# Shift and scale of the first norm in four tiles of 512 columns, each followed by its early projection units

## The chip, the cores and the metric

The kernel runs on one core of a Trainium2 chip. The core has TensorE (PE: matmuls; its weight loads are listed as PEld), VectorE (DVE), ScalarE (ACT), GpSimd (POOL) and SyncE (SP, which here only issues DMAs), and 16 DMA engines that move data between HBM and the on-chip memory. Each engine works through its own queue in order and waits at an instruction until the semaphores of that instruction are met. The metric is the device time of one execution in microseconds.

## The reference

One layer of a decoder trunk on 256 tokens of width 2048, in float32: a mixer with four groups of attention heads, and a mixture of 16 experts. Only the beginning matters here:

```python
c_act = silu(c)                                   # (1, 2048)
mod = c_act @ ada_w + ada_b                       # (1, 12288)
sh1, sc1, g1, sh2, sc2, g2 = split(mod, 6)
h = rmsnorm(x, norm1_g) * (1 + sc1) + sh1         # (256, 2048)
x = x + g1 * token_mixer(h, w_in, ...) 
h = rmsnorm(x, norm2_g) * (1 + sc2) + sh2
x = x + g2 * moe_ffn(h, ...)
return rmsnorm(x, final_g)
```

`token_mixer` multiplies h with w_in (2048 rows) and `moe_ffn` runs every token through two of 16 experts; all experts' weights are read, 201 MB of the 368 MB that come from HBM. The shift sh1 and the scale sc1 are each a product of one row with a 2048 x 2048 matrix (16.8 MB each).

## The kernel before

**Order of the work.** Weights come through one stream of units of 512 KB (class `Stream`): a list `units`, in which each entry has a key and a DMA that SyncE issues. They go through a ring of 11 slots (RING). `stream.get` hands out a unit, `stream.done` gives its slot back, and the next unit of the list is then issued into that slot; later more buffers join the free list. The instructions of the program are then put in order for each engine by a scheduler that works with an estimate of its own, so the rows of an engine's queue don't stand in the order of the source.

**The first stage** computes the hidden activations h, transposed, in 16 tiles k of 128 rows by 256 tokens, and starts the projection with w_in as soon as tiles of h exist.

- `ada_acc` (lines 457 to 475) computes a tile of shift or scale: for each unit it multiplies the row silu(c) (spread over 32 columns, `cB`) with 128 rows of ada_w. Four matmuls for four k go to four column groups of TensorE at a time (`tile_position`), and ScalarE copies the sums out into `ada_ev`. In the trace a float32 matmul has two records, so that four matmuls make two packs of four.
- `ada_cols` (lines 488 to 504) adds the four groups and turns the row into columns: the column matmuls (tile `ada_c`, L498), a transpose on VectorE (L500), and the bias (L501).
- `hidden` (lines 599 to 604): hs = xT * A1 + B1 on VectorE, the high half Hh on ScalarE, the low half Hl on VectorE.
- `halves` (lines 555 to 566) splits a unit of w_in into high and low parts, whi on ScalarE (L560, 1048 ns) and wlo on VectorE (L562, 1225 ns). There are two buffers of each (SPLITS).
- `early_mms` and `early_mms5` multiply such a unit with the tiles of h: three matmuls of 256 columns for each product (lines 537 to 539), 24 for a unit, into accumulators that stay in PSUM. 16 units of the first kind (`uwe`, one k each, 1024 columns of w_in) and 7 of the second (`uw`, four k each, 256 columns) are done in this stage: 552 matmuls.
- `x_transposes` (lines 592 to 597) makes xT, and `bias_tiles` (lines 525 to 532) makes the tables of the relative-position bias, 16 small matmuls a time, and needs nothing else.

Shift and scale come in eight tiles of 256 columns, that is two k each. A unit of such a tile holds 512 rows of 256 columns, in pieces of 1 KB. The loop over j (lines 606 to 637) does a scale tile, then a shift tile, then `hidden(j)`, and sets the early units of the tiles before in between. Behind the stage come the gates of the fourth head group (`gacc`, L680), the rest of the projection, attention, the output projection, the router, and from about 563 us on the experts in pairs.

Of the kernel before, what the change touches and what calls it, by code (L numbers as in the profile page):

```python
# [36 lines left out]
SIXTH = 6  # L37
ATAG = "ada"
# [111 lines left out]
def hybrid_trunk_kernel(  # L150
# [34 lines left out]
    def ada_units(col, key, n, kn):  # L185

        def mk(u):
            return lambda t: nc.sync.dma_start(
                t.rearrange("p (k n) -> p k n", k=kn), adaT[:, kn * u:kn * u + kn, col:col + n])
        return [((key, u), mk(u)) for u in range(KC // kn)]  # L190
# [8 lines left out]
    def win_units(i):  # L199
        m, kind, j, col = wtiles[i]  # L200
        if kind == "g":
            return [((("w", i), 0), lambda t: nc.sync.dma_start(
                t[:, 0:384].rearrange("p (k n) -> p k n", k=KC), winT[:, :, col:col + 24]))]

        def mk(u):
            return lambda t: nc.sync.dma_start(
                t.rearrange("p (k n) -> p k n", k=4), winT[:, 4 * u:4 * u + 4, col:col + 256])
        return [((("w", i), u), mk(u)) for u in range(4)]
# [43 lines left out]
    def early_unit(k):  # L252
        return (("we", k), lambda t: nc.sync.dma_start(t, winT[:, k, 3840:4864]))
# [1 line left out]
    acol = {"sh1": 0, "sc1": 2048, "g1": 4096, "sh2": 6144, "sc2": 8192, "g2": 10240}  # L255

    def ada_tile(key):
        return ada_units(acol[key[0]] + 256 * key[1], key, 256, 4)

    def ada_block(key):  # L260
        nm, b, width = key
# [4 lines left out]
                                              [(nm, 2 * h, 512), (nm, 2 * h + 1, 512)])]  # L266

    units = []
    for j in range(8):
        units += ada_tile(("sc1", j))  # L270
        if j == 0:
            units += [(None, lambda t=t: nc.sync.dma_start(x0[t], x[0, 128 * t:128 * t + 128, :])) for t in range(2)]
        units += [early_unit(2 * j)] + ada_tile(("sh1", j)) + [early_unit(2 * j + 1)]
        if j % 2:
            units.append(win_units(4)[j // 2])
        elif j:
            units.append(win_units(SIXTH)[j // 2 - 1])

    nw = len(wtiles)
    wkeys = [u[0] for i in range(NEARLY, nw) for u in win_units(i)[3 * (i == SIXTH):]]  # L280
# [287 lines left out]
    def early_split(k):  # L568
        esp[k] = halves(stream.get(("we", k)))
        stream.done(("we", k))  # L570

    def early_mms(k):
        hi, lo = esp.pop(k)
        for i in range(4):
            for cc in range(2):
                c0 = 256 * i + 128 * cc
                three(early[i][:, cc, :], hi[:, c0:c0 + 128], lo[:, c0:c0 + 128], Hh[:, k, :], Hl[:, k, :],
                      False, k == KC - 1 and cc == 1, True)
# [24 lines left out]
            A.copy(Hh[:, k, :], hs[:])  # L603
            V.tensor_tensor(Hl[:, k, :], hs[:], Hh[:, k, :].bitcast(F32), OP.subtract)

    for j in range(8):
        ev = None
        for u in range(4):
            ev = ada_acc(("sc1", j), [u], ev, 4, 256)
        if j == 0:  # L610
            norm1()
        else:
            early_mms(2 * j - 2)
        x_transposes(2 * j)
        bias_tiles(2 * j)
        ada_cols(ev, 2, A1[:, 2 * j:2 * j + 2], 16 + 2 * j, g1n[:, 2 * j:2 * j + 2], tag=ATAG)
        early_split(2 * j)
        ev = None
        for u in range(4):
            ev = ada_acc(("sh1", j), [u], ev, 4, 256)  # L620
        bias_tiles(2 * j + 1)
        ada_cols(ev, 2, B1[:, 2 * j:2 * j + 2], 2 * j, tag=ATAG)
        hidden(j)
        if j:
            early_mms(2 * j - 1)
        if j and j % 2 == 0:
            early_mms5(4, j // 2 - 1)
        early_split(2 * j + 1)
        if j % 2:
            if j > 1:  # L630
                early_mms5(SIXTH, j // 2 - 1)
            early_split5(4, j // 2)
        elif j:
            early_split5(SIXTH, j // 2 - 1)
    for k in (14, 15):
        early_mms(k)
    early_mms5(4, 3)


    qkv = {}  # L640
# [567 lines left out]
    i = -1  # L1208
# [434 lines left out]
```

## Time and profile before

| | us |
|---|---|
| median of 3 runs (lowest, highest) | 1061.38 (1059.71, 1063.89) |
| the profiled execution | 1063.05 |
| its span, first to last instruction | 1061.3 |
| busy in the span: TensorE | 965.6 (91%) |
| VectorE | 516.6 (49%) |
| ScalarE | 330.6 (31%) |
| data moved | 371.18 MB, mean 350 GB/s |

The profile gives for each engine the time in which it executes something; waiting is idle time. Matmuls overlap, and their ends are modelled, so that the distance between starts tells more than the duration of one. The granted clock (PEclk) is the share of TensorE's 2.4 GHz that it was allowed; 0.50 is 1.2 GHz. The DMA share is the sum of the packets' times over the 16 engines and can come out a little over 1. Tiles are named with the stream's names: `usc` and `ush` are units of the scale and the shift, `uwe` and `uw` units of w_in.

### The profile page before, as it was taken

The numbers are of one execution on the slowest core, as the hardware profiler recorded it, in microseconds if no ns is written. First come the engines' busy times: TensorE is split into PE (matmuls) and PEld (weight loads), VectorE is DVE, ScalarE is ACT, GpSimd is POOL, SyncE is SP. The second block draws the span as 40 slices with busy tenths as digits, with TensorE's granted clock in tenths as the row PEclk, the third lists the DMA queues.
The fourth block names the chain that finished last, engine by engine and source line by source line (L and its number), as shares of the span: only waits on it lengthen the run. The fifth ranks groups of instructions, "written<-read, shape, count | busy, mean of one in ns | idle before, by whom it ended". The sixth has DMA issues, their size and how long they took to land.

```text
span 1061.3 us, 16623 instructions
## 1 busy us (share of the span) xinstructions
PE 965.6 (91%) x6433; PEld 587.5 (55%) x6433; DVE 516.6 (49%) x1093; ACT 330.6 (31%) x710; POOL 4.8 (0%) x14
## 2 busy tenths in 40 slices
PE   5999989899889999979998999999989896998884
PEld 1677778898778986646794434433343332432222
DVE  2444557996899999544345232414133130413115
ACT  3333334455565757634334100100020000200013
POOL 0000000000000000000000000000000000000000
PEclk9999999899989999989998999999999999999997
DMA  9999999996999999999743999999999999999994
GB/s 330 356 358 358 353 318 304 332 360 217 318 352 327 334 348 385 349 304 382 274 150 114 410 408 409 409 409 409 409 409 409 409 408 409 409 410 409 409 387 135
DMA packets 172031, 371.18 MB, mean 350 GB/s; under 512 B 13561, under 2 KB 92322, under 8 KB 171690
## 3 DMA queue, kind: packets, MB, share of 16 engines
q1 hardware_dynamic: 170944, 368.42, 94.6%
q10 hardware_dynamic: 938, 1.61, 0.4%
q8 instruction: 53, 0.87, 0.3%
q14 instruction: 32, 0.26, 0.1%
q0 software_dynamic: 64, 0.02, 0.0%
HBM read 367.91 MB, written 2.10 MB: 349 GB/s over the span
## 4 chain that ended last, share of the span: by engine, by line
PE 57%; DMA 28%; DVE 8%; ACT 3%; issue 3%; SPq 0%; DVEq 0%; ACTq 0%
DMA ugu<-in_exp_w_up_dram 10%; DMA ugu<-in_exp_w_gate_dram 7%; PE dn L170 7%; PE acc L537 5%; PE acc L538 4%; PE acc L539 4%; DMA udh<-in_exp_w_down_dram 4%; PE ada L170 3%; PE gatep L170 3%; PE upp L170 3%; PE oacc L541 3%; PE oacc L542 3%; PE oacc L543 3%; DMA uw<-in_w_in_dram 2%; PE pg L1381 2%
## 5 line engine op out<-in xcount | busy, mean ns | idle before, releaser
L537 PE MATMUL acc<-Hh,wlo 128*128 128x256 f32 x512 | 148.2, 300 | 6.6 <-DVE wlo L562 4.2
L538 PE MATMUL acc<-Hl,whi 128*128 128x256 f32 x512 | 147.4, 290 | 0.0
L539 PE MATMUL acc<-Hh,whi 128*128 128x256 f32 x512 | 146.6, 289 | 0.0
L173 PE MATMUL gatep<-ugu,xg 128*64 128x512 f32 x364 | 122.6, 600 | 0.0
L173 PE MATMUL upp<-ugu,xg 128*64 128x512 f32 x368 | 121.2, 595 | 0.0
L170 PE MATMUL dn<-udh,heT 128*64 128x512 f32 x242 | 112.1, 600 | 2.9 <-DVE heT L1451 2.6
L537 PEld LDWEIGHTS acc<-Hh,wlo 128*128 128x128 f32 x512 | 98.7, 198 | 18.9 <-DVE wlo L562 6.7
L173 PE MATMUL dn<-udh,heT 128*64 128x512 f32 x234 | 108.3, 600 | 0.0
L538 PEld LDWEIGHTS acc<-Hl,whi 128*128 128x128 f32 x512 | 100.2, 196 | 3.4 <-issue 2.9
L539 PEld LDWEIGHTS acc<-Hh,whi 128*128 128x128 f32 x512 | 99.7, 195 | 2.5 <-issue 2.2
L1434 DVE TENSOR_TENSOR he<-upp,sg 128x128 f32<-128x128 f32 x32 | 7.1, 284 | 170.6 <-PE upp L173 167.9
L562 DVE TENSOR_TENSOR wlo<-uw,whi 128x1024 fp32r<-128x1024 f32 x62 | 75.7, 1221 | 15.8 <-ACT whi L560 15.6
L170 PE MATMUL gatep<-ugu,xg 128*64 128x512 f32 x144 | 75.2, 611 | 7.6 <-DMA ugu<-in_exp_w_gate_dram 7.6
L170 PE MATMUL upp<-ugu,xg 128*64 128x512 f32 x144 | 73.6, 600 | 7.8 <-DMA ugu<-in_exp_w_up_dram 7.8
L560 ACT CAST whi<-uw 128x1024 fp32r<-128x1024 f32 x62 | 64.8, 1047 | 48.7 <-PE acc L539 21.4
L1464 DVE TENSOR_TENSOR xt<-xt,sco 128x512 f32<-128x512 f32 (+1 forms) x70 | 42.3, 639 | 54.7 <-PE sco L1463 54.2
L1513 ACT CAST yhl<-yo 128x512 fp32r<-128x512 f32 x31 | 19.2, 618 | 159.7 <-DVE yo L1507 153.3
L170 PEld LDWEIGHTS dn<-udh,heT 128*64 128x64 f32 x242 | 30.0, 136 | 62.1 <-issue 49.1
L562 DVE TENSOR_TENSOR wlo<-uo,whi 128x1024 fp32r<-128x1024 f32 x31 | 37.8, 1223 | 51.2 <-ACT whi L560 49.4
L541 PE MATMUL oacc<-wlo,Oh 128*128 128x512 f32 (+1 forms) x160 | 57.8, 362 | 0.0
L542 PE MATMUL oacc<-whi,Ol 128*128 128x512 f32 (+1 forms) x160 | 56.0, 350 | 0.0
L543 PE MATMUL oacc<-whi,Oh 128*128 128x512 f32 (+1 forms) x160 | 55.9, 350 | 0.0
(397 smaller groups left out, 1730.0 us busy)
## 6 DMA issues: line engine op xcount, KB each, us to landing
ugu<-in_exp_w_up_dram SPq DMA_DIRECT2D x128, 512.0 KB, 10.2
ugu<-in_exp_w_gate_dram SPq DMA_DIRECT2D x127, 512.0 KB, 10.2
udh<-in_exp_w_down_dram SPq DMA_DIRECT2D x119, 512.0 KB, 10.2
usc<-in_ada_w_dram SPq DMA_DIRECT2D x64, 512.0 KB, 7.8
ush<-in_ada_w_dram SPq DMA_DIRECT2D x62, 512.0 KB, 7.1
uw<-in_w_in_dram SPq DMA_DIRECT2D x62, 512.0 KB, 6.0
ug<-in_ada_w_dram SPq DMA_DIRECT2D x56, 512.0 KB, 7.2
uo<-in_w_out_dram SPq DMA_DIRECT2D x31, 512.0 KB, 9.6
```

Of the source, the lines that this page charges most:

```text
L170: ins = op(*args, **kw).ins
L173: ins = op(*args, **kw).ins
L537: ins = mm(o, wl, hh, start=first, stop=False)
L538: mm(o, wh, hl, start=False, stop=False)
L539: mm(o, wh, hh, start=False, stop=last)
L541: ins = mm(o, hh, wl, start=first, stop=False)
L542: mm(o, hl, wh, start=False, stop=False)
L543: mm(o, hh, wh, start=False, stop=last)
L560: A.copy(hi, w)
L562: V.tensor_tensor(lo, w, hi[:].bitcast(F32), OP.subtract)
L1381: mm(pg[:, i, :], x_[:, t, i, 128 * c:128 * c + 128], oh4[q][:, t].rearrange("p e s -> p (e s)"), start=n == 0, stop=n == 3)
L1464: V.tensor_tensor(y(t, cs), y(t, cs), o, OP.add)
```

## The change

The tiles of shift and scale become 512 columns wide, four of each. A unit of 512 KB then holds 256 rows of 512 columns, in pieces of 2 KB, and `ada_acc` takes two units at a time, since four k are needed for the four column groups. In the stream, all 16 units of a tile's scale and shift now come first, and its four units `uwe` and one or two units `uw` follow. The early work becomes a generator, `early_work(j)`, of which the loop takes one piece after each two units of shift or scale of the next tile; what is left is taken before `hidden`. The numbers of matmuls in the early work, of transposes, of bias tiles and of bytes stay as they are.

```diff
     def ada_tile(key):
-        return ada_units(acol[key[0]] + 256 * key[1], key, 256, 4)
+        return ada_units(acol[key[0]] + 512 * key[1], key, 512, 2)
...
-    for j in range(8):
+    for j in range(4):
         units += ada_tile(("sc1", j))
...
-        units += [early_unit(2 * j)] + ada_tile(("sh1", j)) + [early_unit(2 * j + 1)]
-        if j % 2:
-            units.append(win_units(4)[j // 2])
-        elif j:
-            units.append(win_units(SIXTH)[j // 2 - 1])
+        units += ada_tile(("sh1", j)) + [early_unit(k) for k in range(4 * j, 4 * j + 4)]
+        units += [win_units(i)[j] for i in (4, SIXTH)[:2 - (j == 3)]]
...
-    for j in range(8):
+    def early_work(j):
+
+        for k in range(4 * j, 4 * j + 4):
+            early_split(k)
+            yield
+            early_mms(k)
+        for i in (4, SIXTH)[:2 - (j == 3)]:
+            early_split5(i, j)
+            yield
+            early_mms5(i, j)
+        yield
+
+    work = iter(())
+    for j in range(4):
         ev = None
-        for u in range(4):
-            ev = ada_acc(("sc1", j), [u], ev, 4, 256)
+        for u in range(0, 8, 2):
+            ev = ada_acc(("sc1", j), [u, u + 1], ev, 2, 512)
+            next(work, None)
...
+        for _ in work:
+            pass
+        hidden(2 * j)
+        hidden(2 * j + 1)
+        work = early_work(j)
```

How the queues move, at three places. First SyncE at the start of the program: before, four units of the scale, x, one unit of w_in and four units of the shift.

```order
L188 DMA usc_94<-in_ada_w_dram 128x4x256
L188 DMA usc_96<-in_ada_w_dram 128x4x256
L188 DMA usc_98<-in_ada_w_dram 128x4x256
L188 DMA usc_100<-in_ada_w_dram 128x4x256
L272 DMA x_76<-in_x_dram 128x2048
L272 DMA x_77<-in_x_dram 128x2048
L253 DMA uwe_104<-in_w_in_dram 128x1024
L188 DMA ush_106<-in_ada_w_dram 128x4x256
L188 DMA ush_108<-in_ada_w_dram 128x4x256
L188 DMA ush_110<-in_ada_w_dram 128x4x256
L188 DMA ush_112<-in_ada_w_dram 128x4x256
L253 DMA uwe_114<-in_w_in_dram 128x1024
```

Now eight units of the scale stand ahead of x, and the shift's units follow; these are its rows from x on.

```order
L272 DMA x_76<-in_x_dram 128x2048
L272 DMA x_77<-in_x_dram 128x2048
L188 DMA ush_112<-in_ada_w_dram 128x2x512
L188 DMA ush_114<-in_ada_w_dram 128x2x512
L188 DMA ush_116<-in_ada_w_dram 128x2x512
L188 DMA ush_202<-in_ada_w_dram 128x2x512
L188 DMA ush_204<-in_ada_w_dram 128x2x512
L188 DMA ush_212<-in_ada_w_dram 128x2x512
L188 DMA ush_210<-in_ada_w_dram 128x2x512
L253 DMA uwe_220<-in_w_in_dram 128x1024
L188 DMA ush_218<-in_ada_w_dram 128x2x512
L253 DMA uwe_228<-in_w_in_dram 128x1024
```

The first unit of w_in has moved from behind x to behind the seventh unit of the shift, and the first four shift units from place 10 to 13 to places among 13 to 21.

Second, TensorE at the end of a shift tile. Before, behind the column matmuls (`ada_c`) of the fifth shift tile:

```order
L498 MATMUL ada_c<-ada_ev,kc 32x64 x4
L170 MATMUL ada<-usc_779,cB 32x256
L173 MATMUL ada<-usc_779,cB 32x256 x3
L596 MATMUL xtr<-ident,x_76 128x128
L596 MATMUL xtr<-ident,x_77 128x128
L596 MATMUL xtr<-ident,x_76 128x128
L596 MATMUL xtr<-ident,x_77 128x128
L537 MATMUL acc<-Hh,wlo 128x256 x4
L170 MATMUL ada<-usc_785,cB 32x256
L173 MATMUL ada<-usc_785,cB 32x256 x3
```

Now, behind those of the second shift tile; the bias matmuls (`S<-tabs,line`) go on like this to 16 of them:

```order
L173 MATMUL ada<-ush_523,cB 32x512 x2
L495 MATMUL ada_c<-ada_ev,kc 32x128 x4
L526 LDWEIGHTS line
L526 MATMUL S<-tabs,line 128x32
L526 LDWEIGHTS line
L526 MATMUL S<-tabs,line 128x32
```

and these rows follow the sixteenth:

```order
L526 LDWEIGHTS line
L526 MATMUL S<-tabs,line 128x32
L534 MATMUL acc<-Hh,wlo 128x256 x4
L535 MATMUL acc<-Hl,whi 128x256
L536 MATMUL acc<-Hh,whi 128x256
L534 MATMUL acc<-Hh,wlo 128x256
L535 MATMUL acc<-Hl,whi 128x256
L536 MATMUL acc<-Hh,whi 128x256
```

Before, units of the next scale tile and transposes of x stood between the column matmuls and the next split matmuls; now 16 bias matmuls stand there, and the next scale units come 60 split matmuls later or more.

Third, VectorE behind the third shift tile, from the transpose of the columns on (`hs` is the hidden tile before it is split, `Hl` its low half):

```order
L497 STREAM_TRANSPOSE ada_ev<-ada_c 128x128
L498 TENSOR_TENSOR B_173<-ada_ev,rT 128x4
L599 TENSOR_SCALAR hs<-xT,A_172,B_173 128x256 x2
L529 COPY TA<-S 128x16x8
L559 TENSOR_TENSOR wlo<-uwe_1003,whi 128x1024
L601 TENSOR_TENSOR Hl<-hs,Hh 128x256 x2
L529 COPY TC<-S 128x16x8
L599 TENSOR_SCALAR hs<-xT,A_172,B_173 128x256 x2
L559 TENSOR_TENSOR wlo<-uw_1041,whi 128x1024
L601 TENSOR_TENSOR Hl<-hs,Hh 128x256 x2
```

Four tiles of `hs` are now made one after another where there were two, and a bias copy (TA) and a split (wlo) stand between the first two and their low halves.

## Rows read from the trace of the kernel before

**Rows 1.** Busy time of each engine in stretches of the span, with the number of instructions; then granted clock, DMA share and GB/s.

```profile
63.00:147.00 84.00, 78.90 (x943) 60.31 (x940) 38.60 (x87) 29.58 (x57) 0.31 (x1) 1.00 1.05 343
160.00:200.00 40.00, 36.54 (x375) 32.42 (x364) 33.69 (x71) 17.04 (x32) 1.05 (x2) 0.91 0.96 320
200.00:240.00 40.00, 40.00 (x335) 36.26 (x336) 38.41 (x72) 21.83 (x52) 0.00 (x0) 1.00 0.99 345
520.00:580.00 60.00, 55.86 (x367) 45.18 (x367) 32.79 (x77) 27.06 (x53) 0.00 (x0) 0.91 0.42 141
600.00:1000.00 400.00, 369.99 (x1690) 141.99 (x1684) 105.54 (x205) 36.58 (x61) 0.00 (x0) 0.99 1.03 409
```

In each row: the stretch, its length, and the busy times of PE, PEld, DVE, ACT and POOL in that order.

**Rows 2.** Groups of TensorE's matmuls from 63 to 147 us: count, busy time, mean ns of one, idle time before them and what ended most of it.

```profile
L538 PE MATMUL acc<-Hl,whi 128*128 128x256 f32 x120 | 34.0, 290 | 0.0
L539 PE MATMUL acc<-Hh,whi 128*128 128x256 f32 x120 | 33.4, 286 | 0.0
L537 PE MATMUL acc<-Hh,wlo 128*128 128x256 f32 x120 | 32.5, 293 | 0.1
L170 PE MATMUL ada<-usc,cB 128*32 128x256 f32 x40 | 12.0, 390 | 2.5 <-DVE ada_ev L500 2.5
L498 PE MATMUL ada_c<-ada_ev,kc 128*32 128x64 f32 x83 | 3.4, 231 | 1.1 <-ACT ada_ev L474 1.1
```

**Rows 3.** Timeline of TensorE in the same stretch: start, duration.

```profile
86.52 0.28 PE L538 MATMUL acc<-Hl,whi 128*128 128x256 f32 x1
86.64 0.28 PE L539 MATMUL acc<-Hh,whi 128*128 128x256 f32 x1
86.85 0.40 PE L170 MATMUL ada<-usc,cB 128*32 128x256 f32 x1
...
87.09 0.38 PE L170 MATMUL ada<-usc,cB 128*32 128x256 f32 x1
...
87.42 0.39 PE L538 MATMUL acc<-Hl,whi 128*128 128x256 f32 x1
87.64 0.28 PE L539 MATMUL acc<-Hh,whi 128*128 128x256 f32 x1
...
94.01 0.38 PE L170 MATMUL ada<-ush,cB 128*32 128x256 f32 x1
...
94.22 0.38 PE L170 MATMUL ada<-ush,cB 128*32 128x256 f32 x1
```

**Rows 4.** Waits of SyncE's queue from 25 to 147 us: who was waited for, us in total, times, longest.

```profile
SPq L188 <- PE ada L173: 30.6, 26, 6.2
```

**Rows 5.** Timeline of TensorE: the gate matmuls behind the early work.

```profile
159.39 1.93 PE L680 MATMUL gacc<-Hh,uw 128*24 128x256 f32 x32
```

**Rows 6.** DMA from 63 to 130 us, in all and by issues (count, size, median us from issue to landing), and the stretch 400 to 420 us as in rows 1.

```profile
DMA packets 20618, 23.87 MB, mean 356 GB/s; under 512 B 722, under 2 KB 19512, under 8 KB 20609
ush<-in_ada_w_dram SPq DMA_DIRECT2D x17, 512.0 KB, 8.3
usc<-in_ada_w_dram SPq DMA_DIRECT2D x16, 512.0 KB, 9.5
uwe<-in_w_in_dram SPq DMA_DIRECT2D x8, 512.0 KB, 8.6
uw<-in_w_in_dram SPq DMA_DIRECT2D x4, 512.0 KB, 9.6
400.00:420.00 20.00, 19.07 (x134) 13.07 (x132) 19.80 (x49) 14.76 (x35) 0.00 (x0) 1.00 1.05 387
```

**Rows 7.** The start: a shift transfer in the chain of waits (start, duration), the first steady split matmul in the timeline, and a group of split matmuls from 31 to 42.6 us, the first of the three lines.

```profile
11.61 11.92 DMA ush<-in_ada_w_dram
...
33.53 0.39 PE L538 MATMUL acc<-Hl,whi 128*128 128x256 f32 x1
...
L537 PE MATMUL acc<-Hh,wlo 128*128 128x256 f32 x16 | 4.7, 331 | 0.0
```

**Rows 8.** Timeline of TensorE at the gate g1 of the mixer, whose tiles have 512 columns already: start, duration.

```profile
440.56 0.59 PE L170 MATMUL ada<-ug,cB 128*32 128x512 f32 x1
...
440.98 0.59 PE L170 MATMUL ada<-ug,cB 128*32 128x512 f32 x1
```

**Rows 9.** Timeline of all engines behind the last shift tile; in brackets the idle time before and what ended it.

```profile
146.65 0.32 PE L498 MATMUL ada_c<-ada_ev,kc 128*32 128x64 f32 x8 [0.54 <-ACT ada_ev L474]
...
149.13 1.17 PE L537 MATMUL acc<-Hh,wlo 128*128 128x256 f32 x4 [2.17 <-ACT Hh L603]
...
150.06 1.23 DVE L562 TENSOR_TENSOR wlo<-uw,whi 128x1024 fp32r<-128x1024 f32 x1 [0.53 <-ACT whi L560]
150.10 0.41 PE L538 MATMUL acc<-Hl,whi 128*128 128x256 f32 x1
...
150.31 0.42 PE L539 MATMUL acc<-Hh,whi 128*128 128x256 f32 x1
```

**Rows 10.** Four short stretches, columns as in rows 1: the two with idle time, and the two behind them.

```profile
146.20:149.10 2.90, 0.32 (x8) 0.16 (x8) 1.72 (x5) 0.80 (x3) 0.00 (x0) 1.00 1.19 308
149.50:152.50 3.00, 3.00 (x16) 3.00 (x16) 2.48 (x4) 0.83 (x2) 0.00 (x0) 0.50 1.05 379
43.80:46.00 2.20, 0.77 (x9) 0.31 (x10) 2.17 (x7) 0.93 (x2) 0.00 (x0) 1.00 1.09 348
46.90:50.00 3.10, 3.10 (x32) 2.29 (x32) 1.37 (x4) 0.97 (x3) 0.00 (x0) 0.50 1.06 362
```

More of the change, by code (lines that the diff above doesn't have):

```diff
@@ L604, in hidden @@
             V.tensor_tensor(Hl[:, k, :], hs[:], Hh[:, k, :].bitcast(F32), OP.subtract)
-    for j in range(8):
+    def early_work(j):
[10 more added lines that the diff above has]
+    for j in range(4):
         ev = None
-        for u in range(4):
-            ev = ada_acc(("sc1", j), [u], ev, 4, 256)
+        for u in range(0, 8, 2):
+            ev = ada_acc(("sc1", j), [u, u + 1], ev, 2, 512)
+            next(work, None)
         if j == 0:
             norm1()
[L612 to L617, printed above, removed]
-        ev = None
[L619 to L637, printed above, removed]
+        x_transposes(4 * j)
+        x_transposes(4 * j + 2)
+        bias_tiles(4 * j)
+        bias_tiles(4 * j + 1)
+        ada_cols(ev, 4, A1[:, 4 * j:4 * j + 4], 16 + 4 * j, g1n[:, 4 * j:4 * j + 4], tag=ATAG)
+        ev = None
+        for u in range(0, 8, 2):
+            ev = ada_acc(("sh1", j), [u, u + 1], ev, 2, 512)
+            next(work, None)
+        bias_tiles(4 * j + 2)
+        bias_tiles(4 * j + 3)
+        ada_cols(ev, 4, B1[:, 4 * j:4 * j + 4], 4 * j, tag=ATAG)
+        for _ in work:
[3 more added lines that the diff above has]
+        work = early_work(j)
+    for _ in work:
+        pass
     qkv = {}
```

## The prediction

> **What bounds the kernel now.** I read the views in this order: the busy time by stretches, the groups of TensorE in one stretch, the timeline of TensorE instruction by instruction, and SyncE's waits. The change touches the first 160 of 1061.3 us only, so the question is what paces that stage and whether a shift of its end reaches the end of the program.
>
> The stretches [rows 1] show two engines at their limit at once. From 63 to 147 us TensorE is busy 78.90 of 84 us and the DMA engines have a share of 1.05. The groups [rows 2] say what fills TensorE: 360 split matmuls (three lines of 120), the matmuls of shift and scale, the bias tiles. The idle time ahead of them is small: 2.5 us before the first matmul of a scale tile, 1.1 us before the column matmuls, 5.1 us in all (84 less 78.90). The timeline [rows 3] confirms that this is no artefact of long modelled ends: split matmuls start every 0.12 us, and the shift and scale matmuls every 0.24 or 0.22 us in packs of four, without a hole. So TensorE has next to no slack, and SyncE agrees: its longest wait in this stage is for TensorE to release a shift or scale buffer, 30.6 us in 26 waits [rows 4]. DMA is full as well, but any gain in its rate makes it the one that waits.
>
> Behind it, a shift of this stage is kept: 160 to 200 us has TensorE at 36.54 and VectorE at 33.69 of 40, 200 to 240 us has 40.00 and 38.41 [rows 1]. From 520 to 580 us DMA mostly idles (share 0.42), as the expert pass has not begun, and from 600 to 1000 us it streams expert weights at 409 GB/s with a share of 1.03 [rows 1]. That block of fixed length starts when the early and middle stages are done. A microsecond won or lost at 160 us therefore moves the end by about one.
>
> **The change part by part.** The marker for the sum is the gate matmul at 159.39 us [rows 5], which in both orders stands right behind the early projection work.
>
> *Transfers.* The 64 units of shift and scale go from rows of 1 KB to rows of 2 KB. From 63 to 130 us 45 units (23.87 MB) moved [rows 6]; 8 of them have rows of 4 KB, as the expert weights have, and at 409 GB/s take 1.28 us each; the other 37 are left 56.7 us, 1.5 us each. From 400 to 420 us, where all units have rows of 2 KB, 387 GB/s [rows 6] makes 1.35 us. So 64 x 0.15 = 9.9 us of DMA time go away. I count none of it: TensorE has only the 5.1 us of idle time to give, and those are counted below.
> The Trainium skill, "DMA: Bandwidth & Descriptors" (Specifications), puts the least transfer for line rate at 512 B; by it 1 KB and 2 KB rows are equally fast and this term would be 0 in place of 9.9. The trace disagrees, 356 against 387 GB/s; with the rule, the faster rival below would lose half its chance.
>
> *Start.* The first shift tile is complete only after 16 units, not 8. Before, its third unit lands at 23.53 [rows 7], the fourth 1.5 us later at 25.0, and the split matmuls run steadily from 33.53, 8.5 us behind. Now 8 more units precede (8 x 1.35 = 10.8) and the old 8 are cheaper (8 x 0.16 = 1.3): 34.5, and steady from 43.0. By then the kernel before has done 48 split matmuls [rows 7], 16 on each of the three lines up to 42.6 us, the changed one 5; both have done 16 units of shift and scale. 43 x 0.118 = 5.1 us behind, less one group of bias matmuls that the new order has already done (0.5): **+4.6 us**.
>
> *Matmuls of shift and scale.* Half as many, twice as wide. At 512 columns packs start 0.42 us apart [rows 8], twice the 0.22 of 256 columns, so the columns cost the same: 0. What is saved is changing over between kinds of work. In [rows 3] the step from a split matmul to a scale one is 0.21 in place of 0.12, the step back 0.33 in place of 0.22 to 0.24, and the next split matmul follows after 0.22 in place of 0.12: 0.3 us for two changes. In the order of the two programs I count 107 changes between 42.6 us and the last early matmul before, 67 after: 40 x 0.15 = **-6.0 us** (half to one and a half times that are my bounds).
>
> *Tile boundaries.* Before, the first matmuls of the next scale tile and the transposes of x stand behind the column matmuls of a shift tile and cover most of the way from shift to hidden activations; the five boundaries from 63 to 147 us leave the 5.1 us of idle time. Now the early work is drained before `hidden` and the next tile's work needs the fresh hidden tiles: the order shows only 16 bias matmuls (0.5 us) in between. The price of the uncovered way is in the trace, at the last boundary, where nothing covers it before either [rows 9]: column matmul at 146.65, first split matmul at 149.13 after 2.17 us idle, and steady flow only from 150.10, when the low half Hl exists; that is 2.7 us beyond the column matmul, 2.2 with the bias matmuls off. It comes twice more (after the second and third shift tile; the last boundary is in both kernels, the first in the start term), and at the third VectorE's order puts a bias copy and a split (1.23 us in rows 9) ahead of Hl, 1 us more: 2 x 2.2 + 1.0 = **+5.4 us**. If the covers hold after all it is 0; with four splits ahead of Hl it would be 9. In exchange the old idle time goes: 5.1 less two evictions of a shift tile that nothing covers now (0.9 each, the idle 0.54 of rows 9 with the wider copy) = **-3.3 us**.
>
> *Clock.* After the 2.17 us at 147 the granted clock was 0.50 from 149.5 to 152.5, and after idle time at 43.8 to 46.0 it was 0.50 from 46.9 to 50.0 [rows 10]; split matmuls then start 0.21 apart in place of 0.12 [rows 9]. Each such stretch gives back half of its 3.4 us. Two new boundaries make 0 to 3.4; as they are shorter than the one at 147 I take one: **+1.7 us**. The stretch at the start is in both.
>
> *Slots.* The ring has 11. Six units (four early, two of w_in) now wait together for the hidden tiles while the next tile's shift and scale must come through the other five; SyncE's queue is in order, and a scale unit that waits for a buffer freed by the last of the early splits holds back four shift units. A unit takes 8.3 to 9.5 us from issue to landing in a full queue [rows 6]. For each of the two later tiles I bound the stall by 0 and 3 us, and take 0.75: **+1.5 us**.
>
> *Tail.* Behind the last shift tile there are 120 early split matmuls, not 72, but the 48 are missing earlier: 0.
>
> Sum: 4.6 - 6.0 + 5.4 - 3.3 + 1.7 + 1.5 = +3.9 us. On the profiled execution, 1063.05 us (span 1061.3 and 1.75 around it), that is 1066.95. It lies 1.67 above the median of 1061.38, so the forecast is 1065.3, told as 1065.
>
> **The rivals.** *A, faster: transfers were the pace.* If the boundaries hide (the first Hh comes before the bias matmuls are through) and the slots never stall, the sum is 4.6 - 6.0 - 3.3 = -4.7, and with 1.5 times the saving at changes -7.7: 1054 to 1057. For it: the DMA share of 1.05 and 9.9 us of room. Against it: the dense starts of rows 3.
> The Trainium skill, "Trainium Kernel Development and Optimization" (the paragraph on reading a trace), calls matmul busy time a bad metric and weight-load busy share a good one; by it TensorE stands at 72% from 63 to 147 us (60.31 of 84 in rows 1), has slack, and rival A would be the forecast. The starts 0.12 us apart in rows 3 do not bear this out: a matmul could not have started in between.
>
> *B, nothing arrives:* VectorE does two more of its weighted sums inside the TensorE-bound tail and so has 2 x 1.28 us less to do in the stretch after 180 us where it is the pace; with less stalling at the slots (-1.5) the +3.9 becomes 0: 1061.
>
> *C, much slower: the ring starves.* Each of the three tiles after the first waits for units that could only be issued once the last early split freed its slot, 3 us each, and each wait brings a stretch at half clock: 3 x (3 + 1.7) - 1.5 - 1.7 = +10.9 on top of 3.9 less the hidden share of the boundaries (about 4): 1072. It decides as soon as the head of SyncE's queue is held for more than the 3.9 us by which the transfers of a tile (16 x 1.35 + 4 x 1.28 + 2 x 1.5 = 29.7 us) are shorter than TensorE's 33.6 (84 us for two and a half). For it: the in-order queue, and 8 to 9 us from issue to landing; against it: those 3.9 us.
>
> **How the numbers follow.** A change of less than 0.5% (5.3 us) can't be told from none here. The forecast has 0.50 and its own range is 1061 to 1070; A 0.16, B 0.14, C 0.20. Faster by over 0.5% (under 1056.1) is most of A: 0.14. Slower (over 1066.7) is C and 0.4 of the forecast: 0.41. The rest, 0.45, is no change. The range, 1055 to 1074, takes in all of B, most of A and the nearer half of C.
>
> **What would show it.** Right: the changed profile has split matmuls starting later than 40 us, idle time of 2 us or more on TensorE at three boundaries some 34 us apart waiting for Hh, DMA share under 1 before 150 us while SyncE waits, and the gate matmul 2 to 6 us later than 159.39. Wrong: the gate matmul before 157 us (A); the gate matmul late but the router's matmuls on time (B); TensorE waiting for shift or scale transfers for several us in each tile (C). A granted clock of 1.00 across the new boundaries would take out the clock term.

## The result and the profile after

| | before | after |
|---|---|---|
| median, us (lowest, highest) | 1061.48 (1059.71, 1063.89) | 1077.11 (1075.7, 1079.51) |
| the profiled execution | 1063.05 | 1075.7 |
| its span | 1061.3 | 1073.9 |

The ratio is 1.0143 [1.012, 1.0167]: the change costs 15.6 us. That is slower, as the forecast's sign had it, but four times its +3.9 us, and above its range.

The busy time of after by stretches, columns as in [rows 1]; the last row shows the 25 us that begin 20 us behind its gate matmul; the row of before for the same place stands with e14 below.

```profile
34.00:160.00 126.00, 110.71 (x1063) 83.34 (x1063) 60.04 (x115) 43.15 (x79) 0.31 (x1) 0.95 0.94 328
63.00:147.00 84.00, 74.32 (x732) 52.10 (x724) 35.28 (x74) 28.36 (x53) 0.31 (x1) 0.98 0.92 323
160.00:200.00 40.00, 35.28 (x351) 31.54 (x350) 27.15 (x41) 13.73 (x23) 0.53 (x1) 0.91 0.96 313
200.00:240.00 40.00, 36.33 (x306) 32.69 (x300) 34.98 (x82) 19.68 (x45) 0.53 (x1) 0.96 0.84 275
520.00:580.00 60.00, 55.55 (x352) 47.25 (x352) 31.34 (x68) 28.15 (x53) 0.00 (x0) 0.96 0.57 199
600.00:1000.00 400.00, 371.23 (x1710) 144.68 (x1708) 107.76 (x213) 38.77 (x65) 0.00 (x0) 0.99 1.03 409
184.10:209.10 25.00, 21.20 (x184) 19.23 (x184) 15.87 (x39) 8.47 (x19) 0.53 (x1) 0.86 0.85 277
```

Two things differ from [rows 1]. From 63 to 147 us TensorE has lost 4.6 us of busy time to idle time and DMA is no longer full (0.92 in place of 1.05). And from 160 to 240 us VectorE is busy 62.1 us in place of 72.1, and from 200 to 240 TensorE 36.33 in place of 40.00: the work behind the early stage is the same in both programs, so here the engines wait. The expert block runs as before (409 GB/s).

The timeline of TensorE in after: the start, the three later boundaries between a shift tile's columns and the hidden tiles, and the gate matmul.

```profile
43.50 1.44 PE L534 MATMUL acc<-Hh,wlo 128*128 128x256 f32 x5
44.73 0.54 PE L535 MATMUL acc<-Hl,whi 128*128 128x256 f32 x1
...
75.79 0.43 PE L495 MATMUL ada_c<-ada_ev,kc 128*32 128x128 f32 x8 [0.74 <-ACT ada_ev L471]
77.81 0.74 PE L534 MATMUL acc<-Hh,wlo 128*128 128x256 f32 x4 [1.10 <-ACT Hh L600]
...
113.37 0.74 PE L534 MATMUL acc<-Hh,wlo 128*128 128x256 f32 x4 [0.84 <-ACT Hh L600]
114.94 0.58 PE L535 MATMUL acc<-Hl,whi 128*128 128x256 f32 x1 [0.83 <-DVE Hl L601]
...
147.26 0.74 PE L534 MATMUL acc<-Hh,wlo 128*128 128x256 f32 x4 [2.29 <-ACT Hh L600]
148.56 0.55 PE L535 MATMUL acc<-Hl,whi 128*128 128x256 f32 x1 [0.57 <-DVE Hl L601]
...
164.10 1.93 PE L684 MATMUL gacc<-Hh,uw 128*24 128x256 f32 x32
```

The gate matmul comes at 164.10 in place of 159.39 [rows 5], 4.7 us later. The program ends 12.6 us later. Two thirds of the loss in this execution appear behind the marker. Shifts against before at later milestones: the compressed keys (tile kcT on VectorE) 190.09 against 181.01, +9.1; parts of the values on TensorE 198.48 against 184.46, +14.0; the first softmax 207.01 against 191.29, +15.7; the router (its first matmul on TensorE, tile rt) 510.8 against 497.3, +13.5. From the router on next to nothing changes any more.

What happens between the compressed keys (+9.1) and the first softmax (+15.7) stands in TensorE's timeline of after from 190 us. The 4.4 us between the gate matmul and the keys were not separated.

```profile
190.62 0.67 PE L781 MATMUL z<-dcv,ident 128*64 128x128 f32 x8 [2.52 <-DVE kcT L813]
...
193.91 0.58 PE L534 MATMUL acc<-Hh,wlo 128*128 128x256 f32 x1
194.29 0.41 PE L535 MATMUL acc<-Hl,whi 128*128 128x256 f32 x1
194.50 0.41 PE L536 MATMUL acc<-Hh,whi 128*128 128x256 f32 x1
...
198.13 0.41 PE L535 MATMUL acc<-Hl,whi 128*128 128x256 f32 x1
198.48 1.71 PE L795 MATMUL part<-uw1v,blk 128*32 128x128 f32 x32
```

In before the same place reads:

```profile
181.54 0.68 PE L777 MATMUL z<-dcv,ident 128*64 128x128 f32 x8 [0.58 <-DVE kcT L809]
182.15 1.97 PE L828 MATMUL scmp<-kcT,qkD 128*128 128x30 f32 x16
184.05 0.49 PE L170 MATMUL sp<-qkD 64*128 64x128 f32 x2
184.46 1.08 PE L791 MATMUL part<-uw1v,blk 128*32 128x128 f32 x32
```

In after 20 split matmuls of the projection stand ahead of part<-uw1v, and as they follow 2.52 us of idle time they start 0.21 apart, which is half clock. VectorE's waits from 160 to 215 us show who pays, first in after, then in before.

```profile
DVE ada_v L481 <- DMA usc<-in_ada_w_dram: 6.7, 3, 2.9
DVE parts L799 <- PE part L795: 4.1, 1, 4.1
```

```profile
DVE kcT L809 <- PE kcp L805: 3.7, 1, 3.7
```

VectorE's queue is in order, and behind the copy of parts stand the compressed values, the next splits and the weighted sums that free slots of the ring. The change touches none of these instructions; the scheduler has put them in another order. Behind the early stage the order differs at 473 of TensorE's 3681 places, 164 of VectorE's 848, 96 of ScalarE's 493 and 44 of SyncE's 608, all within the first 1261, 270, 183 and 57 places (to about 330 us).

So there were two candidates: the early stage itself, and the order behind it, which the change moved only by way of the scheduler.

### The profile page after: what moved, and what is told of

Same layout as the page of the kernel before. It is cut to its first block, busy times and chain, and to the rows that moved or that the text cites. A ratio compares the mean times of both kernels' runs of the same rounds, so it can differ in the third digit from the quotient of the medians.

```text
span 1073.9 us, 15917 instructions
## 1 busy us (share of the span) xinstructions
PE 962.1 (90%) x6113; PEld 581.4 (54%) x6113; DVE 515.2 (48%) x1073; ACT 328.7 (31%) x702; POOL 4.8 (0%) x14
## 4 chain that ended last, share of the span: by engine, by line
PE 58%; DMA 25%; DVE 9%; ACT 4%; issue 3%; SPq 0%; DVEq 0%; ACTq 0%
PE dn L170 8%; DMA ugu<-in_exp_w_gate_dram 7%; DMA ugu<-in_exp_w_up_dram 7%; DMA uw<-in_w_in_dram 4%; PE acc L534 4%; PE acc L535 4%; PE gatep L170 4%; PE acc L536 4%; PE upp L170 3%; PE ada L170 3%; PE pg L1385 3%; PE oacc L538 3%; DMA udh<-in_exp_w_down_dram 3%; PE oacc L539 3%; PE oacc L540 3%
## 5 line engine op out<-in xcount | busy, mean ns | idle before, releaser
L534 PE MATMUL acc<-Hh,wlo 128*128 128x256 f32 x512 | 150.6, 299 | 11.1 <-DVE wlo L559 6.8
L536 PE MATMUL acc<-Hh,whi 128*128 128x256 f32 x512 | 148.9, 292 | 0.0
L1438 DVE TENSOR_TENSOR he<-upp,sg 128x128 f32<-128x128 f32 x32 | 7.1, 283 | 170.5 <-PE upp L173 167.8
L170 PEld LDWEIGHTS dn<-udh,heT 128*64 128x64 f32 x242 | 30.0, 136 | 62.1 <-issue 49.0
```

The source lines that it names most:

```text
L170: ins = op(*args, **kw).ins
L534: ins = mm(o, wl, hh, start=first, stop=False)
L536: mm(o, wh, hh, start=False, stop=last)
```

## The experiments

Differences in us are against the median of before that was measured beside each run (1061.55 to 1062.67).

**The order of early work, with the order behind left to the scheduler.** In e1 the early units of w_in stand between the scale and shift units of the next tile, in the order of their use; in e3 the last pieces of early work are held back until `hidden` is issued.

```diff
...
-        units += ada_tile(("sh1", j)) + [early_unit(k) for k in range(4 * j, 4 * j + 4)]
-        units += [win_units(i)[j] for i in (4, SIXTH)[:2 - (j == 3)]]
+        for nm in ("sc1", "sh1"):
+            for n, un in enumerate(ada_tile((nm, j))):
+                units.append(un)
+                if n % 2 and ew:
+                    units.append(ew.pop(0))
...
```

> The changed kernel with its stream in order of use: the early units of w_in stand between the scale and shift units behind which they are split, instead of ahead of all of them. Theory R (ring): the six waiting units starve the stream (DMA share 0.76 at 60 to 70 us and at 90 to 100 us) and the late units then hold up VectorE behind the stage. R expects a DMA share of 1.0 or more from 30 to 130 us, the gate matmul at 161 us or earlier instead of 164.1, and 1066 to 1071 us in all. Theory V (VectorE's order): the loss behind the stage is made by weighted sums that stand ahead of kcT in VectorE's order and wait for their units there (11 sums in the changed kernel, 9 before, 10 here). V expects the gate perhaps earlier, but some 7 us more lost between it and the end of the compressed keys, and over 1072 us in all.

```diff
-            next(work, None)
+            if u < 2:
+                next(work, None)
...
-        for _ in work:
-            pass
         hidden(2 * j)
         hidden(2 * j + 1)
+        for _ in work:
+            pass
```

> The changed kernel, but of the early work of a tile the last one or two pieces are held back until the next hidden tiles are issued, so that 24 to 48 split matmuls cover the way from shift to hidden. The forecast's boundary term (2 x 2.2 us uncovered) expects the gate matmul 3 to 5 us earlier, at 159 to 161 us, and the idle time ahead of the first split matmul of a tile gone at the two inner boundaries. With it VectorE's order behind the stage has changed too (9 sums ahead of kcT instead of 11): V expects 1062 to 1067 us. R, with the ring as starved as before, expects 1070 us or more.

Measured: e1 1070.19, 1.0072 [1.0048, 1.0096]; e3 1070.42, 1.007 [1.0045, 1.0095]. Both win 7 us on after. But both had their order behind planned anew too, so they tell nothing yet about the early stage.

In e2 three of VectorE's weighted sums are tied behind the tiles that waited; the early stage is that of after. In e4 the tiles are 256 columns wide again, with the generator of the change; its edit is shown against after.

```diff
+        first = {9: "parts_k", 10: "blk_v", 12: "parts_v"}.get(len(summed))
+        if first:
+            behind(ins.ins, fixed[first].ins)
```

> The changed kernel with the order of VectorE tied where the compressed keys are made: the ninth weighted sum behind the copy of parts (k), the tenth behind blk (v), the twelfth behind parts (v), as in the kernel before. Nothing else changes, the early stage is that of the changed kernel. V expects the gate matmul at 164.1 as before this tie, kcT at about 187 instead of 190.1, and 1069 to 1072 us in all, 5 to 8 us won. R expects the units to be late all the same, so that other instructions wait for them: within 3 us of 1077.

```diff
-    for j in range(4):
+    for j in range(8):
...
-        for u in range(0, 8, 2):
-            ev = ada_acc(("sc1", j), [u, u + 1], ev, 2, 512)
+        for u in range(4):
+            ev = ada_acc(("sc1", j), [u], ev, 4, 256)
```

> The new order of the early work (generator, units of w_in behind both the scale and the shift of their tile, drained ahead of hidden) with the old eight tiles of 256 columns and rows of 1 KB. It tells the width from the order. If the width makes the loss (a start 11.8 us later, six units held in the ring): first split matmul at 33 us as before, DMA share 1.05 throughout, gate matmul at 160 to 163 us because seven boundaries stand uncovered, 1062 to 1066 us in all. If the order makes it: 164 us or later at the gate and 1070 us or more.

Measured: e2 1079.87, 1.0159 [1.0126, 1.0193]; e4 1079.37, 1.0151 [1.0111, 1.0191]. The tie moved far more than the three sums (in the traces some 330 of VectorE's last 848 rows differ from before, against some 130 in after), so e2 did not test what it was made for. And e4, narrow as before, is no faster than after: in its profile the gate matmul is 0.9 us late and the router 15.8. Width can't be the whole cause, and no edit can be judged as long as the order behind moves with it.

**Early stage and order behind, crossed.** From here on the order behind is held: a table names, for each engine, the place of each instruction in the other kernel's order, and edges without a semaphore hold it.

```diff
+        for name, text in PINNED.items():
+            own = [i for i in traced if str(i.engine) == "EngineType." + name]
...
+            for p, n in zip(places, places[1:]):
+                tc.add_manual_dep(own[n], own[p].name, mybir.DependencyInfo(
+                    mybir.DependencyClass.NoSync, mybir.DependencyReason.DATA), reason="order")
```

The early stage of after with the order behind of before is e6, and again e19 on another chip. The early stage of before with the order behind of after is e7. The early stages of e1, e3 and e4 with the order behind of before are e8, e15 and e10.

> The early stage of the changed kernel with the order of the kernel before, on all engines, for everything behind it (the instructions behind the early stage are the same ones in both kernels; 473 of TensorE's 3681 and 164 of VectorE's 848 stand at another place). Theory O (order behind): the change loses only what its early stage loses, 4.7 us at the gate matmul, and the rest of its 15.7 us comes from the new order of the work behind. O expects the gate at 163 to 166 us, the first router matmul 339 us behind it or less as before (338), and 1065 to 1068 us in all. R (late units stall whatever order): more than 343 us from gate to router and 1072 us or more.

> The counterpart: the early stage of the kernel before, unchanged, with the changed kernel's order behind it. O expects the gate matmul at 159 to 160 us as before and 5 to 10 us lost between it and the router, 1066 to 1071 us in all. R expects that with the units as early as before nothing waits longer: 1061 to 1064 us.

> The changed kernel with its stream in order of use (first run of this study), and the order of the kernel before for all work behind the early stage. O expects the gate at 165 us as in that run and its end 338 us or a little less further on: 1064 to 1069 us. R expects the fuller stream to show here: at least 3 us less than the run with the old middle and the changed kernel's own stream.

> Eight tiles of 256 columns with the new order of the early work, as in the fourth run, and the order of the kernel before behind the early stage. With the order behind taken out, this and the run with the old middle and four tiles differ in the width alone. If the early loss (8.9 us there) is the width's (later start, longer and uncovered boundaries, slower clock behind them), this one has its gate matmul at 160 to 161 us and takes 1062 to 1065 us. If it is the order of the early work: 1068 us or more.

> The third run's early stage (one or two pieces of early work held back to cover the way from shift to hidden) with the old order behind. If the uncovered boundaries are what remains of the early loss (5 us), 1065 to 1067 us instead of 1070.8. If the late start carries it, 1069 us or more.

| early stage | order behind planned for it | order behind of before |
|---|---|---|
| before | | 1061.5 |
| after | 1077.11, 1.0143 [1.012, 1.0167] | e6 1070.78, 1.0076 [1.0048, 1.0104] |
| after, another chip | | e19 1072.79, 1.0093 [1.0061, 1.0125] |
| order of use | e1 1070.19 | e8 1070.09, 1.0075 [1.0049, 1.0101] |
| held back | e3 1070.42 | e15 1071.8, 1.0108 [1.0082, 1.0134] |
| narrow, new generator | e4 1079.37 | e10 1062.1, 1.0008 [0.9992, 1.0025] |

With the early stage of before, the order behind of after alone costs 8.7 us (e7 1070.64, 1.0078 [1.0051, 1.0104]). With after's early stage it costs 4.7 to 6.7 (15.6 less 10.9 and 8.9); after's interval lies above that of e6 and meets that of e19 at its edge. In e4 it cost 17.3, in e1 nothing. This part is the scheduler's and has no fixed size.

The 8.7 us of e7 are not simply a part of after's loss. In e7 the first gate matmul waits for ScalarE, which in the order of after does two copies and a split ahead of the activations that the gate matmul waits for:

```profile
PE gacc L716 <- ACT qkD L772: 3.5, 1, 3.5
```

After has no such wait: its gate matmul starts 0.2 us behind the last early one.

The rest, 8.9 to 10.9 us, is the early stage's. It goes away with the width and what follows from it (e10 is before again), and neither the order of the stream (e8) nor the place of the held pieces (e15) changes it by more than the intervals. Of the expectations, e7 came out as theory O had it and e10 as the width had it; e6 lies between its two, and e8 a microsecond above the one of O. The gain of e1 and e3 on after was wholly the order behind.

**Which part of the order behind.** Three kernels have the early stage of before. In e12 only VectorE's places 29 to 49 stand as in after (two more weighted sums ahead of kcT). In e14 also 42 split matmuls stand ahead of the compressed values, 20 of them ahead of part<-uw1v. In e11 the whole chain stands as in after: the first 270 instructions behind the stage on TensorE, 50 on VectorE, 34 on ScalarE, 25 on SyncE. The edit is the table alone.

> As the last, but only 21 places of VectorE's order are the changed kernel's, from the copy of parts (k) to the maximum of the compressed scores: two more weighted sums stand ahead of kcT, a third and two more splits ahead of parts (v). TensorE keeps the order of before, so the 20 split matmuls stay behind the first layer of the compressed values (part<-uw1v). V in its first form (the sums that wait for their units make the loss) expects 1065 us or more. If the 20 split matmuls ahead of part<-uw1v are what costs: 1060 to 1064 us.

> The kernel before, with 42 split matmuls moved ahead of the last matmuls of the compressed values (vcp), 20 of them ahead of part<-uw1v, and the 21 places of VectorE's order that belong to them (as in the twelfth run, which cost nothing). If these matmuls hold up the compressed values and with them all of the first head group, as theory O now says: 1069 to 1074 us, first layer of the values 8 us later or more, as in the run with the whole chain new (1073.7). If the places ahead of it make the loss: 1064 us or less.

> The early stage of the kernel before and its order behind, except for the first 270 instructions of TensorE behind the stage and what belongs to them (50 of VectorE, 34 of ScalarE, 25 of SyncE): these stand as in the changed kernel. They end with the compressed values (vcp) and the softmax over the compressed keys. If the 8.7 us of the run with the new middle are lost there, 1068 to 1072 us and 8 us or more later at the first scores; if it is the order after them, 1063 us or less.

Measured: e12 1061.63, 0.9995 [0.9977, 1.0013]; e14 1066.33, 1.0047 [1.0025, 1.0069]; e11 1073.66, 1.011 [1.0082, 1.0138]. The sums cost nothing. The split matmuls ahead of the compressed values cost 4.8 us, less than expected. The profile of e14 fell on its slowest execution (1073.78; the others 1062.03 to 1070.39), so it shows the mechanism larger than the median has it: TensorE's timeline, VectorE's waits from 160 to 215 us, and the 25 us that begin 20 us behind the gate matmul.

```profile
193.24 1.21 PE L907 MATMUL part<-uw1v,blk 128*32 128x128 f32 x32
```

```profile
DVE parts L911 <- PE part L907: 4.6, 1, 4.6
DVE ada_v L600 <- DMA usc<-in_ada_w_dram: 4.5, 2, 3.0
DVE prob L1021 <- PE sp L289: 2.9, 1, 2.9
```

```profile
179.30:204.30 25.00, 17.61 (x145) 15.70 (x144) 14.88 (x38) 7.30 (x17) 0.53 (x1) 0.79 0.61 205
```

The wait of VectorE for parts is that of after (4.6 and 4.1 us). What holds the transfers in this profile stands in SyncE's waits from 178 to 206 us: the unit at the head of its queue waits 12.1 us for the same product.

```profile
SPq L304 <- PE part L907: 12.1, 1, 12.1
```

The DMA share is 0.61, where before has 0.93 in a window at the same place of its program:

```profile
179.40:204.40 25.00, 21.54 (x196) 19.00 (x195) 22.20 (x55) 10.58 (x22) 0.52 (x1) 0.86 0.93 314
```

In after the longest such wait of SyncE is 3.0 us and the share 0.85; e12, which costs nothing, has 7.0 us and 0.84. So e14 shows that the place of the split matmuls can cost time, but not that after loses its time by way of the transfers.

The other 6.8 us of e11 were not separated further; its profile has the 3.5 us wait of the gate matmul that e7 has, and after has not. That e11 takes longer than e7, whose whole order is that of after, is within the intervals.

**The wide early stage.** In e9 the first 512 columns come as two tiles of 256, which undoes the late start; the order behind is that of before here and in all that follows. In e13 ten matmuls of zeros, added into an accumulator, stand behind each shift tile's columns, to fill the boundary. They add work and no value.

```diff
+    TILES = ((0, 2), (2, 2), (4, 4), (8, 4), (12, 4))
```

> The start undone: the first 512 columns in two tiles of 256 columns, the other 1536 in three tiles of 512, early work in the changed kernel's order, and the order of the kernel before behind the early stage. The forecast's start term (4.6 us) expects split matmuls from 31 to 34 us and the gate matmul at 159 to 161 us, so 1060 to 1064 us in all. If the start was not what the early stage lost, the gate stays at 164 us or later.

```diff
+        for _ in range(10):
+            tc.keep_in_program_order(mm(early[0][:].rearrange("p c n -> p (c n)"), zero[:, 0:128], zero[:], start=False, stop=False))
```

> The early stage of the changed kernel with 10 matmuls of zeros (512 columns, added into an accumulator that they leave as it is) behind the column matmuls of each shift tile, and the old order behind. They fill the way from shift to hidden, so TensorE is busy there. If the slower clock behind the boundaries is a part of the early loss, the granted clock stays at 1.00 there, the gate matmul comes 2 to 5 us earlier than in the run with the old middle alone, and the whole takes 1066 to 1068 us instead of 1070.8; if the clock cost nothing, 1070 to 1072 us.

Measured: e9 1068.86, 1.0064 [1.0042, 1.0087]; e13 1069.01, 1.0082 [1.005, 1.0113]. Both intervals overlap that of e6, so neither the start nor the boundaries alone can be seen to be the cost; the start term expected 1060 to 1064 for e9. Both together (e16: e9 with the zeros behind the three wide shift tiles) don't add up either: 1071.28, 1.0093 [1.0074, 1.0112]. In e17, zeros stand at the last boundary of before: 1060.89, 1.0003 [0.9985, 1.0021]. There the half-clock stretch of [rows 10] is gone (granted clock 1.00 from 147 to 160 us) and the time is the same. But in this profile the stretch at the start is longer (0.87 from 34 to 60 us, before 0.93): from 34 to 160 us both have 0.97. So e17 does not show what one stretch costs.

> Start undone and boundaries of the three wide tiles filled with 10 matmuls of zeros each, the old order behind. If start (1.9 us) and clock (1.8 us) add up: 1066 to 1068 us; if they were one and the same thing: 1069 us.

> The kernel before, with the 10 matmuls of zeros at its one uncovered boundary (146.65 to 149.13 us) and the same order behind. If idle time there brings the 3 us at half clock and these cost 1.7 us: clock 1.00 from 149 to 155 us, the gate matmul at 157.5 to 158.5 us and 1060 to 1061 us in all, 1 to 2 us less than before. If the clock falls all the same or its loss is hidden: no change.

The profiles of kernels with one and the same early stage (after, e2, e6, e19) differ more than all that. The stretch from 34 to 160 us in before, e2, e6 and e19, one row each; the granted clock is the third number from the end:

```profile
34.00:160.00 126.00, 117.27 (x1363) 92.00 (x1365) 60.88 (x129) 44.81 (x88) 0.31 (x1) 0.97 1.06 348
```

```profile
34.00:160.00 126.00, 111.39 (x1033) 82.37 (x1032) 58.35 (x113) 42.34 (x78) 0.31 (x1) 0.89 0.91 319
```

```profile
34.00:160.00 126.00, 111.31 (x1014) 82.32 (x1015) 55.86 (x111) 41.73 (x77) 0.31 (x1) 0.88 0.90 313
```

```profile
34.00:160.00 126.00, 111.87 (x1032) 82.81 (x1031) 57.00 (x112) 41.95 (x78) 0.31 (x1) 0.91 0.91 317
```

The row of after stands above. A mean of 0.95 over 126 us is 0.05 x 126 x 2 = 12.6 us at half clock, to about 1.3 us, as the share has two digits. So worked out, before has 7.6, after 12.6, e19 22.7, e2 27.7, e6 30.2 us at half clock, and the gate matmul comes at 159.4, 164.1, 168.3, 167.8 and 170.5. The profile of after is the mildest of the four with its early stage; their mean, 167.7, is +8.3 against before. TensorE's idle time from 25 us to the gate matmul is nearly the same in the four, 16.8 to 17.9 us: what varies is how fast it runs in between.

To test the clock, e18 has the zeros of e13 and also zeros behind each pair of units of the first scale and shift tiles; e19 is its partner without them on the same chip.

> The changed kernel's early stage with the old order behind, and 10 matmuls of zeros behind the column matmuls of each shift tile and behind each pair of units of the first scale and shift tile, where TensorE waits for transfers anyway. If the clock is what the early stage lost beyond the 4 us of the forecast: granted clock 1.00 from 14 us to the gate matmul, which comes at 158 to 161 us, and 1065 to 1067 us in all, 3 to 5 less than e19. If it is not: 1069 to 1071, no less than e19.

> The same kernel as in the run with the old middle (1070.8 us), on the chip of e18, for comparison: 1069 to 1072 us, gate matmul anywhere from 164 to 170 us, by the time at half clock.

```profile
34.00:160.00 126.00, 120.25 (x1141) 87.26 (x1145) 62.52 (x116) 45.20 (x81) 0.31 (x1) 1.00 0.94 327
```

Measured: e18 1067.84, 1.0049 [1.0027, 1.0071], lowest and highest 1063.48 and 1069.12; e19 1072.79, lowest and highest 1067.35 and 1075.78. With the clock at 1.00 the gate matmul comes at 162.16, and 5.0 us are won, though TensorE has more to do. The intervals of the two ratios overlap a little (1.0061 to 1.0071).

What a microsecond at half clock costs can only be estimated. Between the profiles of e6 and e18 it is (170.5 - 162.2) / 30.2 = 0.27. Between e6 and e13 it is 11.9 / 27.7 = 0.43: e13's profile, whose row follows, has a clock of 0.99 (2.5 us at half clock) and the gate matmul at 158.59.

```profile
34.00:160.00 126.00, 119.49 (x1165) 87.76 (x1167) 64.03 (x119) 48.07 (x87) 0.31 (x1) 0.99 0.96 337
```

But e6's profile is its slowest execution, and those of e13 and e18 are their fastest. The record also has the mean granted clock of every execution over its whole span. With each run's mean taken off, the 130 executions of the nineteen runs other than before give 0.13 (standard error 0.03).

By the same record before has 63.7 and 63.8 us at half clock beside e6 and e19, which have 75.3 and 77.4. These 12 to 14 us more make 1.5 to 5.8 us at those prices. So the clock is not most of what the width costs, and two runs say the same: e18 has 50.7 us at half clock, fewer than before, and is still 6.0 us slower than before; e16 has 59.0 against 60.7, and is 9.7 us slower.

What is left does not lie in one place. In the profile of e18 the gate matmul is 2.8 us late and the router 2.3; in that of e13 the gate matmul is 0.8 us early and the router 3.4 late. The other wide kernels with the order of before lose 2.6 to 6.1 us between the two (e10 and e17, both narrow, 1.1 and 0.5). One candidate is that transfers are behind: 61.9 MB were moved by 180 us in before and 62.0 in e10, but 59.8 in after, 57.7 in e6 and 58.3 in e19. Against it stands e18, with 60.6 MB and nothing lost behind the gate matmul. No run changed that alone, so the cause stays open.

## Why the prediction was wrong

**The step that failed** is in the part on what bounds the kernel: a microsecond won or lost at 160 us "moves the end by about one". It took the work behind the marker as fixed. Its instructions are, but their order is not: after's order behind costs 8.7 us on before's own early stage (e7), 5 to 7 on after's. The end of the chain did hold: what is lost at the router, 13.5 us, is lost at the end (12.6). I had compared the queues only at the start, at the boundaries and behind the third shift tile; the 20 split matmuls ahead of part<-uw1v stood in the order of the changed program and could have been read before.

**The sum of the early stage** was right for the profiled execution (+3.9 told, +4.7 found), and less than half of what the kernel with the old order behind really loses (8.9 to 10.9). That agreement is luck: this profile is the mildest of the four with this early stage. The signs that I had named for being right did appear in it (a start behind 40 us, idle time near 2 us or more at three boundaries, a DMA share under 1, a gate matmul 2 to 6 us late), but none of them looked behind the marker. By its terms:

- *Transfers*, 0: DMA left its limit (0.92) and nothing came of the room. (64 x 0.15 is 9.6, not 9.9; nothing hangs on it.) Rival A (faster) fell, and so did B (nothing arrives), as the router is 13.5 us late. The Trainium skill, "Trainium Kernel Development and Optimization" (the paragraph on reading a trace), would, as the prediction read it, have made A the forecast; the result speaks against that reading at a weight-load share of 72%.
- *Start*, +4.6: steady from 44.73, told 43.0. Undoing it in e9 wins 2 to 4 us on e6 and e19, within the intervals; the term is not confirmed in size.
- *Changes of work, boundaries, slots*: idle time of TensorE from 25 us to the gate matmul is 17.9 us in place of 9.7, +8.2, which is what the idle terms make (4.6 + 5.4 - 3.3 + 1.5 = 8.2). Busy time is 3.5 us less; I had told -6.0 and +1.7 for the clock, -4.3. Idle time at the boundaries is 1.84, 2.02 and 3.15 us. SyncE's longest waits from 25 to 165 us are these:

```profile
SPq L188 <- PE ada L173: 29.0, 16, 4.5
SPq L188 <- DVE wlo L559: 13.4, 4, 5.7
```

  Its shift and scale units (L188) wait 13.4 us for splits and 6.0 for Hl, in before 0 and 1.1, as the slots term had it. But e8, in which the splits hold them 9.0 us in place of e6's 19.0, gains nothing on e6. Rival C (the ring starves) had the time nearest to the result, and not its mechanism: in TensorE's waits of the same stretch, shift transfers are 6.9 us in three waits, of which 5.5 is one at the start, not several in each tile.
- *Clock*, +1.7: mis-sized. I took one more stretch of 3.4 us at half clock, at half a microsecond each. The profiles show 5 to 23 us more than in before, varying with the execution; the runs put the price lower, at 0.13 to 0.43, and the whole at 1.5 to 5.8 us.
- *Nothing behind the marker*: the wide kernels lose 2.6 to 6.1 us between the gate matmul and the router even with the order of before (e18 nothing). No term stood for that, and its cause is open.

So 15.6 us are 8.9 to 10.9 of the width and 5 to 7 of the order behind. The first is shown by e6, e10 and e19 together. By which way the width costs them is not shown: the clock is 1.5 to 5.8 us of it by estimate, and start, boundaries and slots could not be told apart. The second is shown in size by after against e6 and e19; e7 shows that this order costs time by itself, but in part by a wait that after has not. No version tried is clearly faster than before.

## What to carry to other kernels

Where a scheduler orders the program, compare the whole order of both programs, behind the edit too, and look for work that is put ahead of a short chain on which another engine's queue stands. To judge an edit, hold the order behind it; the same early stage ran in 1062.1 and 1079.4 us under two orders. Gaps of TensorE can cost more than the idle time itself: in after the split matmuls start 0.21 us apart (half clock) behind two of the three later boundaries, and 0.12 behind the other. And a single profile is one execution: those of e13 and e18 fell on the fastest of their run, those of e6 and e14 on the slowest, so a cost that is read from two profiles needs the other executions beside it.

## What the hardware showed that was not expected

The same early instructions ran with 12.6 to 30.2 us at half clock in four profiled executions, and their end moved by 6.4 us (164.1 to 170.5). Zeros in all gaps of the wide stage kept the clock at 1.00 and seem to win 5.0 us (1067.84 against 1072.79). Zeros at one boundary of before only (e17, 1060.89 against 1061.55) or at the four of the wide stage (e13, 1069.01 against e6's 1070.78) won nothing that stands clear of the noise. So in these runs useless matmuls paid once, and the kernel with them was still slower than before.
